# Weight blocks of three slots, with a new order of the head and of the whole list, in a hand-ordered 3x3 convolution with max pooling

## The chip, the cores and the metric

The kernel runs on one core of a Trainium2 chip. The metric is the device time of one execution in microseconds (us). Three runs of the kernel before took 105.31 to 105.68 us, with a median of 105.47.

## The reference

`x` is 16 x 64 x 64 x 64 (batch, input channels, rows, columns), `weight` is 128 x 64 x 3 x 3, both float32. The output is 16 x 128 x 32 x 32.

```python
x_pad = np.pad(x, ((0, 0), (0, 0), (1, 1), (1, 1)))
for b, co, ci, kh, kw:
    conv[b, co] += weight[co, ci, kh, kw] * x_pad[b, ci, kh:kh+h, kw:kw+w]
output[b, c, i, j] = np.max(conv[b, c, 2*i:2*i+2, 2*j:2*j+2])
```

## The kernel before

**Two ways to make a pair of rows.** The maximum of two neighbouring convolution rows is needed, and the kernel saves matmuls by working on sums and differences of input rows. The work is cut into 32 units: eight pairs of images (two images of 64 channels fill the 128 partitions), four quarters of the height each, eight output rows to a quarter. `SEQ` (line 37) makes 13 of them "K" units and 19 "W" units. A K unit reads bfloat16 rows (`kx`) and needs one row sum (`ks`). A W unit reads float32 rows (`wx`) and needs four row operations that cast as they add or subtract: `we`, `wz`, `wy`, `ws`.

**Products.** A product (line 214) is three matmuls, one for each kernel column, over eight rows of 64 columns, for one image of the pair. It reads 64 partitions (half of the array's rows) with a weight block `wt`, and the products of the two halves (h = 0 and 1) are issued in turn, so that they run side by side in the array. A K unit has the products PAa and PAb into one PSUM bank, PBa and PBb into another, and PR into the second; a W unit has P2 and P0 into one bank, and P3 and P1 into a second one. The names ending in x or a (PAx.0, P1a.18) are half-height parts of the first and the last product. There are eight PSUM banks (`acc`), handed out by number in the list: `PAa.1.0:7` takes bank 7 for unit 1, half 0.

**After the products.** For a K unit ScalarE copies the first bank out (EV), VectorE takes the row maximum with the second (MX), PR adds the common part, ScalarE copies the odd columns out (OD), and VectorE takes the column maximum with the even ones (CM) and stores. For a W unit ScalarE first writes the negated first bank into the second one (SE, line 295), before P0 adds to the first; then ev, mx, P1, od and cm follow in the same way. Row operations are KS (sum of `kx` rows), E or e (`we` on VectorE or on GpSimd), Z (`wz`), Y (`wy`), both on GpSimd, and S (`ws`, VectorE). GpSimd's row operations and some of its other work are held behind the last VectorE operation that reads SBUF alone (`on_gpsimd`, line 81).

**The weights.** `weight` lands as `wraw` (128 output channels on the partitions). From its three kernel rows g0, g1, g2 the head makes seven blocks in bfloat16 in `wq`: D2 = g2 - g1, D0 = g0 - g1, G0, G1, G2, and GM and GP, which are (g0 + g2 - g1) and (g0 + g2 + g1), halved later. TensorE transposes each (`turn`, line 160) into a PSUM bank, and `turn_out` (line 170) copies it to `wt` (on ScalarE line 176, on VectorE lines 178 and 180). A block has four slots of 64 columns, the first one zero, and is turned by four full transposes, each of two neighbouring slots, so that the lower 64 partitions of `wt` hold slot j - 1 and the upper 64 hold slot j; the matmul of half h for kernel column kw therefore reads slot kw - h (line 204).

**Loads.** SyncE's queue carries `wraw`, the first 17 rows of `x` for K unit 0 (`kfirst`, in two parts), the first rows of W unit 0 (`wx`, behind a warm-up matmul), then `ksecond`, the rows of K unit 1 (step KX2, held until D2 is done), further `wx` rows (LD.1 behind GM, LD.2 behind E.0, LD.3 behind E.1, and so on), and the stores. GpSimd's queue carries later K rows (steps L0 to L5, L0 behind KS.0). `kfirst` and `ksecond` are float32 and are cast into `kx`: XO1, XO and XE for the first, X1 (odd rows, needed by PAa.1) and X2 (needed by PBa.1) for the second.

**The order.** Nothing schedules at run time: `ORDER` (line 428) lists every step of all engines as one sequence, and each engine runs its own steps in that order, waiting where data or a bank is missing. `/V`, `/A` and `/P` name VectorE, ScalarE and GpSimd. Two products joined with + are issued matmul by matmul in turn; this text calls such a pair a step of TensorE. Eight warm-up matmuls of 512 columns (line 490) run before the first transpose.

Of the kernel before, what the change touches and what calls it, by code (L numbers as in the profile page):

```python
# [10 lines left out]
def kernel(  # L11
# [8 lines left out]
    nc = tc.nc  # L20
# [109 lines left out]
        nc.gpsimd.memset(t[:, 0, :], 0.0)  # L130
        nc.gpsimd.memset(t[:, H + 1, :], 0.0)

    D2, G0, D0, G2, GM, G1, GP = range(1, 29, 4)
    BLOCKS = {"D2": D2, "G0": G0, "D0": D0, "G2": G2, "GM": GM, "G1": G1, "GP": GP}
    wq = const.tile([CO, 29, CI], BF16)
    wt = const.tile([128, 28, CO], BF16)
    gsum = const.tile([CO, 3, CI], FP32)
    for s in range(0, 29, 4):
        nc.gpsimd.memset(wq[:, s, :], 0.0)
    wv = wraw.rearrange("a (c k) -> a k c", k=K * K)  # L140
    g0, g1, g2 = wv[:, 0:3, :], wv[:, 3:6, :], wv[:, 6:9, :]

# [11 lines left out]
    turned = {}  # L154


    def turned_rows(m):
        return acc.bitcast(BF16)[:, turned[m]]

    def turn(m, bank):  # L160
        t = turned[m] = take(bank)
        unset.add(t)
        for j in range(4):
            nc.tensor.transpose(  # L164
                turned_rows(m)[:, j, :],
                wq[:, BLOCKS[m] - 1 + j : BLOCKS[m] + 1 + j, :].rearrange("a b c -> a (b c)"),
                ident,
            )

    def turn_out(m, engine):  # L170
        free.add(turned[m])
        src = turned_rows(m)[:, 0:4, :]
        dst = wt[:, BLOCKS[m] - 1 : BLOCKS[m] + 3, :]
        half = m in ("GM", "GP")
        if engine is nc.scalar:
            nc.scalar.mul(dst, src, 0.5) if half else nc.scalar.copy(out=dst, in_=src)
        elif half:
            nc.vector.tensor_scalar_mul(out=dst, in0=src, scalar1=0.5)
        else:
            nc.vector.tensor_copy(out=dst, in_=src)  # L180
# [12 lines left out]
    def taps(dst, h, m0, rows, start=False, skip=None, part=(0, R)):  # L193
        lo = h * CI
        i0, i1 = max(part[0], int(skip == 0)), min(part[1], R - int(skip == R - 1))
        made = []
        for kw in (1, 0, 2):
# [3 lines left out]
            made.append(  # L201
                lambda kw=kw, o0=o0, o1=o1, c0=c0, c1=c1: nc.tensor.matmul(  # L202
                    dst[:, i0:i1, o0:o1],
                    wt[lo : lo + CI, m0 + kw - h, :],
                    rows(lo, i0, i1, c0, c1),
                    start=start and kw == 1,
                    stop=True,
# [211 lines left out]
    for name, f in ("ev", evac), ("mx", rowmax), ("od", odd), ("cm", colmax):  # L419
# [6 lines left out]


    ORDER = """
        D0/V g2 g1/P D2 g0 TD0:1 GS/V TD2:4 KX2 XO1/A TG1:0 VD2/V TG0:2 GP/V XO/A TG2:3 VG0/A
        PAx.0.0:6+PAx.0.1:7 GM/V PAa.0.0+PAa.0.1 VD0/A VG1/V LD.1 PAb.0.0+PAb.0.1 XE/V VG2/A TGM:2 KS.0  # L430
        TGP:4 E.0 VGM/A PBa.0.0:0+PBa.0.1:1 EV.0.0 Z.0 VGP/V LD.2 PBb.0.0+PBb.0.1 EV.0.1 P2.0.0:4+P2.0.1:3
        X1/A S.0 L0 PAa.1.0:7+PAa.1.1:2 SE.0.1:5 MX.0.0 Y.0 SE.0.0:6 PAb.1.0+P0.0.1 MX.0.1 X2/A
        P0.0.0+PAb.1.1 E.1 EV.1.0 PR.0.0+PR.0.1 ev.0.1 S.1 LD.3 EV.1.1 PBa.1.0:7+P3.0.1 KS.1 Z.1 OD.0.1
        P2.1.0:2+PBa.1.1:3 OD.0.0 CM.0.1 ev.0.0 mx.0.1 P3.0.0+PBb.1.1 SE.1.0:4 Y.1 PBb.1.0+P2.1.1:1 MX.1.1
        P0.1.0+P1.0.1 CM.0.0 e.2 MX.1.0 SE.1.1:0 P3.1.0+PR.1.1 LD.4 mx.0.0 ev.1.0 PR.1.0+P0.1.1 Y.2 LD.5
        OD.1.1 mx.1.0 od.0.1 P1.0.0+P3.1.1 OD.1.0 CM.1.1 ev.1.1 P1.1.0+P2.2.1:2 cm.0.1 Z.2 od.0.0 mx.1.1
        PAa.2.0:5+PAa.2.1:3 SE.2.1:1 CM.1.0 PAb.2.0+PAb.2.1 L1 od.1.0 cm.0.0 KS.3 PBa.2.0:7+PBa.2.1:6 EV.2.1
        E.3 LD.6 PBb.2.0+P0.2.1 EV.2.0 S.2 LD.7 P2.2.0:3+P1.1.1 KS.2 ev.2.1 Z.3 cm.1.0 PAa.3.0:5+PBb.2.1
        od.1.1 MX.2.0 SE.2.0:2 PAb.3.0+P3.2.1 cm.1.1 Y.3 MX.2.1 PR.2.0+P2.3.1:4 EV.3.0 mx.2.1
        P0.2.0+PAa.3.1:0 OD.2.0 S.3 P2.3.0:5+P1.2.1 ev.2.0 CM.2.0 e.4 P3.2.0+PAb.3.1 od.2.1 SE.3.1:3 cm.2.1  # L440
        PBa.3.0:7+PR.2.1 mx.2.0 SE.3.0:1 Z.4 PBb.3.0+P0.3.1 OD.2.1 P0.3.0+P3.3.1 CM.2.1 ev.3.1 MX.3.0 Y.4
        P1.2.0+PBa.3.1:6 ev.3.0 LD.8 mx.3.1 P2.4.0:4+PBb.3.1 EV.3.1 E.5 od.2.0 PR.3.0+P1.3.1 SE.4.0:5 KS.4
        cm.2.0 P3.3.0+PAa.5.1:0 Y.5 OD.3.0 MX.3.1 od.3.1 P0.4.0+PAb.5.1 mx.3.0 P3.4.0+PR.3.1 Z.5 cm.3.1
        ev.4.0 P1.3.0+P2.4.1:2 EV.5.1 mx.4.0 OD.3.1 PAa.4.0:3+PAa.4.1:4 L2 S.4 SE.4.1:0 PAb.4.0+PAb.4.1
        od.3.0 CM.3.0 Y.6 CM.3.1 P1.4.0+P0.4.1 EV.4.0 cm.3.0 P2.5.0:6+P3.4.1 LD.9 od.4.0 S.5 EV.4.1
        PBa.4.0:3+P2.5.1:7 cm.4.0 e.7 ev.4.1 PBb.4.0+PBa.4.1:1 mx.4.1 SE.5.0:2 PAa.5.0:4+PBb.4.1 SE.5.1:5
        KS.5 MX.4.0 PAb.5.0+P1.4.1 e.6 MX.4.1 P0.5.0+P0.5.1 EV.5.0 PR.4.0+P3.5.1 S.6 ev.5.1 Z.6
        P3.5.0+P2.6.1:4 ev.5.0 mx.5.1 od.4.1 PBa.5.0:7+PR.4.1 OD.4.0 mx.5.0 Y.7 PBb.5.0+P1.5.1 CM.4.0 OD.4.1
        CM.4.1 P1.5.0+PBa.5.1:6 od.5.1 MX.5.0 Z.8 SE.6.1:3 P2.6.0:1+PBb.5.1 cm.4.1 od.5.0 PR.5.0+P0.6.1
        cm.5.0 Z.7 MX.5.1 LD.10 SE.6.0:2 PAa.6.0:0+P3.6.1 cm.5.1 ev.6.1 PAb.6.0+PR.5.1 OD.5.0 e.8 mx.6.1  # L450
        P0.6.0+P2.7.1:4 OD.5.1 EV.6.0 CM.5.1 P3.6.0+PAa.6.1:5 CM.5.0 SE.7.1:0 PAa.7.0:6+PAb.6.1 KS.6 ev.6.0
        S.8 P2.7.0:7+P0.7.1 EV.6.1 S.7 PAb.7.0+P1.6.1 ev.7.1 mx.6.0 L3 PBa.6.0:1+P3.7.1 EV.7.0 Y.8
        P1.6.0+P2.8.1:5 od.6.1 mx.7.1 SE.7.0:4 PBb.6.0+PBa.6.1:6 cm.6.1 od.6.0 e.9 cm.6.0 SE.8.1:3
        P0.7.0+PBb.6.1 MX.6.0 P2.8.0:2+P1.7.1 ev.7.0 LD.11 Z.10 MX.6.1 PR.6.0+P0.8.1 LD.12 SE.8.0:7 LD.13
        P3.7.0+PR.6.1 od.7.1 S.9 ev.8.1 P0.8.0+P3.8.1 Z.9 cm.7.1 mx.7.0 P3.8.0+PAa.7.1:5 ev.8.0 mx.8.1
        P1.7.0+PAb.7.1 OD.6.1 Y.9 OD.6.0 mx.8.0 P2.9.0:0+P1.8.1 EV.7.1 CM.6.0 e.10 P1.8.0+P2.9.1:2 CM.6.1
        od.8.1 SE.9.0:5 cm.8.1 PAa.9.0:1+PBa.7.1:6 SE.9.1:3 S.10 P0.9.0+PBb.7.1 od.8.0 KS.7 od.7.0
        P3.9.0+P0.9.1 cm.8.0 ev.9.0 Y.10 MX.7.1 PAb.9.0+P3.9.1 ev.9.1 mx.9.0 PBa.7.0:7+P2.10.1:0 EV.9.0 Z.11
        mx.9.1 P2.10.0:2+PR.7.1 SE.10.1:1 cm.7.0 PBb.7.0+P1.9.1 E.11 OD.7.1 P1.9.0+P0.10.1 LD.14 CM.7.1
        od.9.1 Z.12 MX.7.0 LD.15 PAa.8.0:4+P3.10.1 od.9.0 cm.9.1 ev.10.1 PR.7.0+PAa.8.1:6 S.11 SE.10.0:3  # L460
        PAb.8.0+PAb.8.1 Y.11 mx.10.1 OD.7.0 P3.10.0+P2.11.1:0 CM.7.0 EV.8.1 cm.9.0 P0.10.0+P1.10.1 L4 KS.8
        SE.11.1:6 S.12 PBa.8.0:7+PBa.8.1:5 ev.10.0 LD.16 E.12 PBb.8.0+P0.11.1 EV.8.0 LD.17 mx.10.0 od.10.1
        Y.13 P2.11.0:2+PBb.8.1 ev.11.1 MX.8.0 P1.10.0+P3.11.1 SE.11.0:4 cm.10.1 Y.12 PR.8.0+PAa.9.1:0 MX.8.1
        od.10.0 P0.11.0+P2.12.1:1 mx.11.1 OD.8.0 Z.13 cm.10.0 P3.11.0+PR.8.1 ev.11.0 CM.8.0
        P2.12.0:3+P1.11.1 OD.8.1 mx.11.0 e.13 SE.12.1:2 PBa.9.0:7+PAb.9.1 CM.8.1 od.11.1 P1.11.0+P3.12.1
        cm.11.1 EV.9.1 KS.9 PBb.9.0+P0.12.1 SE.12.0:6 S.13 od.11.0 P2.13.0:0+PBa.9.1:5 E.14 ev.12.1
        P0.12.0+PBb.9.1 Y.14 cm.11.0 SE.13.0:1 mx.12.1 P3.12.0+P2.13.1:4 ev.12.0 MX.9.1 Z.14 P0.13.0+P1.12.1
        SE.13.1:3 MX.9.0 P3.13.0+PR.9.1 ev.13.0 mx.12.0 e.15 PR.9.0+P0.13.1 OD.9.1 mx.13.0 P1.12.0+P3.13.1
        CM.9.1 OD.9.0 Y.15 ev.13.1 CM.9.0 P1.13.0+P2.14.1:0 od.12.1 mx.13.1 od.12.0 PAa.11.0:4+P2.15.1:5
        od.13.0 Z.15 cm.12.0 SE.14.1:7 PAb.11.0+P1.13.1 cm.12.1 cm.13.0 PAa.10.0:6+P0.14.1 od.13.1 E.16  # L470
        SE.15.1:1 PAb.10.0+P3.14.1 S.15 ev.14.1 P2.14.0:2+P0.15.1 EV.11.0 cm.13.1 S.14 L5 P2.15.0:0+P3.15.1
        ev.15.1 LD.18 e.17 mx.14.1 PBa.10.0:4+PAa.11.1:3 EV.10.0 mx.15.1 SE.14.0:5 PBb.10.0+PAb.11.1
        SE.15.0:6 S.17 P0.14.0+P1.14.1 EV.11.1 KS.10 P0.15.0+P1.15.1 Z.17 MX.10.0 ev.14.0 P3.15.0+PAa.10.1:3
        od.15.1 ev.15.0 cm.15.1 P3.14.0+PAb.10.1 Y.16 od.14.1 mx.15.0 PR.10.0+PBa.10.1:2 EV.10.1 mx.14.0
        Y.17 P2.17.0:0+PBb.10.1 OD.10.0 cm.14.1 P1.15.0+P2.16.1:3 SE.17.0:1 MX.10.1 Z.16 P1.14.0+PAa.12.1:7
        CM.10.0 od.15.0 cm.15.0 P0.17.0+PR.10.1 od.14.0 SE.16.1:4 cm.14.0 P2.16.0:6+PAb.12.1 ev.17.0 S.18
        PBa.11.0:5+P0.16.1 OD.10.1 KS.11 EV.12.1 P3.17.0+P2.17.1:0 S.16 SE.16.0:7 PBb.11.0+P3.16.1 CM.10.1
        e.18 ev.16.1 mx.17.0 P0.16.0+PBa.11.1:2 SE.17.1:3 MX.11.0 P1.17.0+PBb.11.1 Y.18 ev.16.0
        PR.11.0+P0.17.1 MX.11.1 od.17.0 P2.18.0:6+P3.17.1 Z.18 cm.17.0 ev.17.1 mx.16.1 P3.16.0+PR.11.1
        SE.18.0:1 mx.17.1 PAa.12.0:0+P1.16.1 OD.11.0 OD.11.1 KS.12 P0.18.0+P1.17.1 CM.11.1 od.16.1 CM.11.0  # L480
        P3.18.0+P2.18.1:2 cm.16.1 od.17.1 mx.16.0 ev.18.0 PAb.12.0+PBa.12.1:5 SE.18.1:4 mx.18.0
        PBa.12.0:6+PBb.12.1 EV.12.0 cm.17.1 PBb.12.0+P0.18.1 MX.12.1 P1.16.0+P3.18.1 MX.12.0 ev.18.1
        P1a.18.0+PR.12.1 od.16.0 mx.18.1 oda.18.0 cm.16.0 OD.12.1 P1.18.0+P1a.18.1 cma.18.0 PR.12.0+P1.18.1
        CM.12.1 od.18.0 oda.18.1 cm.18.0 od.18.1 cma.18.1 OD.12.0 cm.18.1 CM.12.0
    """

    ones = nc.const_aps.tensor(1.0, [128, 512], BF16)
# [68 lines left out]
```

## Time and profile before

| what | us |
|---|---|
| median of three runs | 105.47 |
| the profiled execution | 105.41 |
| its span | 103.6 |
| TensorE busy | 97.4 of 103.6 |
| VectorE, ScalarE, GpSimd busy | 90.7, 82.0, 67.0 |
| first product (PAx) starts | 6.08 |
| `ksecond` lands | 9.78 |
| PAa.1 starts | 10.47 |
| last product of the unbroken stream ends its part of the chain | 97.52 |

The profile is one execution on the chip, taken by the hardware profiler; times are from the start of its span. The profiled execution took 1.8 us more than its span. PE is TensorE's matmuls, PEld its weight loads, DVE is VectorE, ACT ScalarE, POOL GpSimd and SP SyncE. A row names the line of the kernel, the operation, what it writes <- what it reads with the shapes, how many there are, and in brackets the idle time before it and what ended it. Matmuls are pipelined: a matmul's row is drawn with the time its results take to leave the array, so neighbouring rows overlap, and the distance between two starts is the time that one takes from the other.

### The profile page before, as it was taken

To read this page: it belongs to the slowest core of one execution; us is meant where nothing else is said; L and a number is where in the kernel's file an instruction comes from. 1 tells how busy PE (TensorE), PEld (TensorE's weight loads), DVE (VectorE), ACT (ScalarE), POOL (GpSimd) and SP (SyncE) were. 2 spreads that over 40 slices of the span, in tenths; PEclk is the share of its full clock that TensorE was granted. 3 is DMA by queue.
4 is the path that set the end of the run, shared out by engine and by line. 5 is a ranking of instruction groups with operands and counts; after the bars stand their busy time and mean duration, and the time that the engine had idled before them with its cause. 6 is when DMAs were issued, how large, how long until landed. Compare 5 with 4: busy or idle time off the path is not lost.

```text
span 103.6 us, 2525 instructions
## 1 busy us (share of the span) xinstructions
PE 97.4 (94%) x894; PEld 57.1 (55%) x894; DVE 90.7 (87%) x180; ACT 82.0 (79%) x179; POOL 67.0 (65%) x76
## 2 busy tenths in 40 slices
PE   7998999999999999999999999999999999999920
PEld 2273555555765555555555665655555655666500
DVE  1599979998899899897998999989999999899960
ACT  4478986887988967799879879789889988988530
POOL 7306679847958769968795765984992696770000
PEclk9999999999999999999999999999999999999999
DMA  2976898799998996799899789999948913502362
GB/s 58 348 290 232 213 169 295 227 290 206 368 346 297 160 234 256 229 241 143 194 276 355 280 218 340 168 246 274 366 159 171 272 67 113 191 0 101 108 214 89
DMA packets 12925, 22.81 MB, mean 220 GB/s; under 512 B 1008, under 2 KB 9200, under 8 KB 12912
## 3 DMA queue, kind: packets, MB, share of 16 engines
q1 hardware_dynamic: 11904, 19.63, 56.0%
q0 software_dynamic: 864, 2.88, 19.1%
q8 instruction: 7, 0.11, 0.5%
q10 hardware_dynamic: 144, 0.13, 0.4%
q14 instruction: 6, 0.05, 0.2%
HBM read 17.14 MB, written 8.39 MB: 246 GB/s over the span
## 4 chain that ended last, share of the span: by engine, by line
PE 84%; DMA 7%; DVE 2%; ACT 1%; issue 1%; DVEq 0%
PE acc L202 84%; DMA ksecond<-in_x_dram 5%; DMA wraw<-in_weight_dram 3%; ACT od L304 1%; DVE o L328 1%; DVE wq L395 1%; ACT kx L352 1%; DVE wq L360 0%; DVEq L551 0%
## 5 line engine op out<-in xcount | busy, mean ns | idle before, releaser
L202 PEld LDWEIGHTS <-wt 64*128 64x128 bf16 x858 | 54.4, 94 | 37.3 <-issue 1.3
L202 PE MATMUL acc<-kx,wt 64*128 64x504 bf16 (+5 forms) x318 | 57.5, 369 | 0.4 <-ACT kx L352 0.4
L299 DVE TENSOR_TENSOR acc<-acc,ev 128x512 f32<-128x512 f32 x64 | 42.4, 693 | 3.2 <-PE acc L202 2.2
L290 ACT COPY ev<-acc 128x512 f32<-128x512 f32 x64 | 36.6, 592 | 6.2 <-PE acc L202 5.5
L260 POOL TENSOR_TENSOR wz<-wx 128x512 bf16<-128x512 f32 x19 | 24.1, 1270 | 10.6 <-DVE ks L260 4.4
L202 PE MATMUL acc<-wy,wt 64*128 64x504 bf16 (+1 forms) x114 | 29.6, 377 | 0.0
L202 PE MATMUL acc<-wz,wt 64*128 64x504 bf16 (+1 forms) x114 | 29.2, 377 | 0.0
L202 PE MATMUL acc<-we,wt 64*128 64x504 bf16 (+1 forms) x114 | 29.1, 377 | 0.0
L260 POOL TENSOR_TENSOR wy<-wx 128x512 bf16<-128x512 f32 x19 | 24.1, 1270 | 7.8 <-PE acc L202 3.1
L202 PE MATMUL acc<-ws,wt 64*128 64x504 bf16 (+3 forms) x120 | 28.8, 366 | 0.1
L328 DVE TENSOR_TENSOR o<-acc,od 128x256 f32<-128x256 f32 (+1 forms) x66 | 25.6, 409 | 2.8 <-ACT od L304 2.2
L304 ACT COPY od<-acc 128x256 f32<-128x256 f32 (+1 forms) x66 | 23.3, 375 | 4.5 <-PE acc L202 2.9
L295 ACT ACTIVATE acc<-acc 128x512 f32<-128x512 f32 x38 | 22.0, 586 | 3.4 <-DVE o L328 1.9
L202 PE MATMUL acc<-ks,wt 64*128 64x504 bf16 (+1 forms) x78 | 19.8, 377 | 0.0
L260 POOL TENSOR_TENSOR we<-wx 128x512 bf16<-128x512 f32 x11 | 14.0, 1269 | 5.1 <-PE acc L202 3.4
L260 DVE TENSOR_TENSOR ws<-wx 128x512 bf16<-128x512 f32 x19 | 15.0, 792 | 0.0
L260 DVE TENSOR_TENSOR we<-wx 128x512 bf16<-128x512 f32 x8 | 6.1, 768 | 0.0
L260 DVE TENSOR_TENSOR ks<-kx 128x512 bf16<-128x512 bf16 x13 | 5.4, 419 | 0.1
L105 POOL DMA_DIRECT2D kx<-in_x_dram x6 | 3.5, 589 | 0.0
L490 PE MATMUL acc<-const-bfloat16-1.0 128*128 128x512 bf16 x6 | 2.7, 623 | 0.8 <-PEq L537 0.8
L360 DVE TENSOR_TENSOR wq<-wraw 128x192 bf16<-128x192 f32 x1 | 0.5, 500 | 2.6 <-DMA wraw<-in_weight_dram 2.6
L164 PEld LDWEIGHTS <-wq 128*128 128x128 bf16 x28 | 1.7, 102 | 1.7 <-issue 1.0
(28 smaller groups left out, 18.5 us busy)
## 6 DMA issues: line engine op xcount, KB each, us to landing
out_dram<-o SPq DMA_DIRECT2D x30, 256.0 KB, 4.5
wx<-in_x_dram SPq DMA_DIRECT2D x9, 512.0 KB, 6.6
wx<-in_x_dram SPq DMA_DIRECT2D x5, 480.0 KB, 6.4
wx<-in_x_dram SPq DMA_DIRECT2D x4, 544.0 KB, 6.3
kx<-in_x_dram POOLq DMA_DIRECT2D x3, 496.0 KB, 8.0
kx<-in_x_dram POOLq DMA_DIRECT2D x2, 528.0 KB, 8.9
wx<-in_x_dram SPq DMA_DIRECT2D x1, 576.0 KB, 10.1
ksecond<-in_x_dram SPq DMA_DIRECT2D x1, 512.0 KB, 4.7
```

Source lines behind the costliest of these rows:

```text
L105: return nc.gpsimd.dma_start(out=ktile(i)[:, lo:hi, :], in_=rows_of(p, lo, hi))
L164: nc.tensor.transpose(turned_rows(m)[:, j, :], wq[:, BLOCKS[m] - 1 + j : BLOCKS[m] + 1 + j, :].rearrange("a b c -> a (b c)"), ident,)
L202: lambda kw=kw, o0=o0, o1=o1, c0=c0, c1=c1: nc.tensor.matmul(dst[:, i0:i1, o0:o1], wt[lo : lo + CI, m0 + kw - h, :], rows(lo, i0, i1, c0, c1),
L260: return engine.tensor_tensor(out=r, in0=t[:, f + a : f + a + 2 * R - 1 : 2, :], in1=t[:, f + b : f + b + 2 * R - 1 : 2, :], op=op,)
L290: nc.scalar.copy(out=ev[g], in_=acc[:, ta[g]])
L295: nc.scalar.mul(acc[:, t], acc[:, ta["w", i, h]], -1.0)
L299: nc.vector.tensor_tensor(out=t, in0=t, in1=ev.pop(g), op=MAX)
L304: nc.scalar.copy(out=od[g][:, part], in_=acc[:, tb[g], part, 1::2])
L328: nc.vector.tensor_tensor(out=o[:, h, part], in0=acc[:, tb[g], part, 0::2], in1=od[g][:, part], op=MAX,)
L352: nc.scalar.copy(out=out, in_=in_)
L395: "D2", on_vector(nc.vector.tensor_sub(out=slots(D2), in0=g2, in1=g1))
L490: warm = nc.tensor.matmul(acc[:, n], src[:, 0:128], src, start=True, stop=True, skip_group_check=True)
```

## The change

The blocks of `wq` and `wt` have three slots instead of four, and no zero slot; the memsets of the zero slots on GpSimd are gone. Two full transposes write slots 0 and 1 of a turned block (lower half slot j, upper half slot j + 1). The third slot is made by two transposes of 64 columns: one puts slot 2 into the lower 64 partitions, the other puts slot 0 into the upper 64. A matmul of half 1 reads slot (kw - 1) mod 3. `turn_out` copies 384 columns instead of 512.

```diff
-    D2, G0, D0, G2, GM, G1, GP = range(1, 29, 4)
+    D2, G0, D0, G2, GM, G1, GP = range(0, 21, 3)
...
-    wq = const.tile([CO, 29, CI], BF16)
-    wt = const.tile([128, 28, CO], BF16)
+    wq = const.tile([CO, 21, CI], BF16)
+    wt = const.tile([128, 21, CO], BF16)
...
-    for s in range(0, 29, 4):
-        nc.gpsimd.memset(wq[:, s, :], 0.0)
...
-        for j in range(4):
+        rows, b = turned_rows(m), BLOCKS[m]
+        for j in 0, 1:
             nc.tensor.transpose(
-                turned_rows(m)[:, j, :],
-                wq[:, BLOCKS[m] - 1 + j : BLOCKS[m] + 1 + j, :].rearrange("a b c -> a (b c)"),
-                ident,
+                rows[:, j, :], wq[:, b + j : b + j + 2, :].rearrange("a b c -> a (b c)"), ident
             )
+        nc.tensor.transpose(rows[0:CI, 2, :], wq[:, b + 2, :], ident)
+        nc.tensor.transpose(rows[CI:, 2, :], wq[:, b, :], ident)
...
-        src = turned_rows(m)[:, 0:4, :]
-        dst = wt[:, BLOCKS[m] - 1 : BLOCKS[m] + 3, :]
+        src = turned_rows(m)[:, 0:3, :]
+        dst = wt[:, BLOCKS[m] : BLOCKS[m] + 3, :]
...
-                    wt[lo : lo + CI, m0 + kw - h, :],
+                    wt[lo : lo + CI, m0 + (kw - h) % 3, :],
```

The list `ORDER` is new throughout. Its head, before and after, up to the second step behind PAa.1:

```diff
-        D0/V g2 g1/P D2 g0 TD0:1 GS/V TD2:4 KX2 XO1/A TG1:0 VD2/V TG0:2 GP/V XO/A TG2:3 VG0/A
-        PAx.0.0:6+PAx.0.1:7 GM/V PAa.0.0+PAa.0.1 VD0/A VG1/V LD.1 PAb.0.0+PAb.0.1 XE/V VG2/A TGM:2 KS.0
-        TGP:4 E.0 VGM/A PBa.0.0:0+PBa.0.1:1 EV.0.0 Z.0 VGP/V LD.2 PBb.0.0+PBb.0.1 EV.0.1 P2.0.0:4+P2.0.1:3
-        X1/A S.0 L0 PAa.1.0:7+PAa.1.1:2 SE.0.1:5 MX.0.0 Y.0 SE.0.0:6 PAb.1.0+P0.0.1 MX.0.1 X2/A
+        g1/A D2 D0/V g0 KX2 TD2:2 TG1:0 XO1/V g2 VD2/V TG0:1 GS/V TG2:3 VG0/A XO/V PAx.0.0:6+PAx.0.1:7 GP/P
+        VG1/V XE/A TD0:2 PAa.0.0+PAa.0.1 VD0/A GM/V TGP:1 PAb.0.0+PAb.0.1 KS.0 LD.1 VGP/A E.0 TGM:0 VG2/A
+        PBa.0.0:4+PBa.0.1:2 Z.0 VGM/A LD.2 EV.0.1 PBb.0.0+PBb.0.1 EV.0.0 P2.0.0:1+P2.0.1:3 L0 X1/V MX.0.1
+        SE.0.0:5 PAa.1.0:6+PAa.1.1:0 Y.0 SE.0.1:7 MX.0.0 P0.0.0+PAb.1.1 X2/A S.0 PR.0.0+PR.0.1 EV.1.1 E.1
```

So g1 moves from GpSimd to ScalarE, GP from VectorE to GpSimd, XO1, XO and X1 from ScalarE to VectorE, XE from VectorE to ScalarE; D2 comes ahead of D0; TD0 moves behind PAx, and TGP and TGM stand between products of K unit 0, where before they stood together. In the rest of the list the same products, row operations and evacuations stand in another order and in other banks; of the 19 `we` row operations VectorE has nine (eight before) and GpSimd ten (eleven before). At the end ScalarE's queue issues two of the last stores and SyncE's the others; before it was one.

## The prediction

> **What bounds the kernel now.** I read the page first (busy shares, then the chain that ended last), then the whole chain in order of time, then the timeline of the first 11 us. The page:
>
> ```profile
> span 103.6 us, 2525 instructions
> PE 97.4 (94%) x894; PEld 57.1 (55%) x894; DVE 90.7 (87%) x180; ACT 82.0 (79%) x179; POOL 67.0 (65%) x76
> PE 84%; DMA 7%; DVE 2%; ACT 1%; issue 1%; DVEq 0%
> ```
>
> TensorE is the bound, and the chain in order of time (start, length, what) shows where it is not:
>
> ```profile
> 0.74 3.02 DMA wraw<-in_weight_dram
> ...
> 3.78 0.50 DVE wq L360
> 4.28 0.76 DVE wq L395
> ...
> 5.05 4.72 DMA ksecond<-in_x_dram
> ...
> 9.80 0.63 ACT kx L352
> ...
> 10.47 87.05 PE acc L202 x801
> ```
>
> From 10.47 us TensorE runs 87.05 us without a wait. The changed kernel puts the same matmuls into that stretch, so the result hangs on when it begins and on whether a wait opens in it. Ahead of it: the weights land at 3.76, VectorE makes D0 and only then D2, the load KX2 is held until D2 is done (5.05), lands at 9.78, ScalarE casts it (X1), and PAa.1 starts. TensorE's timeline of that stretch:
>
> ```profile
> 4.42 0.49 PE L164 MATMUL acc<-ident,wq 128*128 128x128 bf16 x4
> 5.08 1.07 PE L164 MATMUL acc<-ident,wq 128*128 128x128 bf16 x16 [0.17 <-DVE wq L395]
> 6.08 1.40 PE L202 MATMUL acc<-kx,wt 64*128 64x256 bf16 x18
> 7.42 0.62 PE L164 MATMUL acc<-ident,wq 128*128 128x128 bf16 x8
> 7.97 1.47 PE L202 MATMUL acc<-kx,wt 64*128 64x512 bf16 x12
> 9.28 0.81 PE L202 MATMUL acc<-we,wt 64*128 64x512 bf16 x6
> 10.47 0.39 PE L202 MATMUL acc<-kx,wt 64*128 64x512 bf16 x2 [0.38 <-ACT kx L352]
> ```
>
> Rows are drawn with their drain, so I read starts, not lengths. A transpose lasts 0.22, so the sixteen start from 5.08 to 5.93: 0.057 apart. The step from the last transpose (5.93) to the first product (6.08) is 0.15, and from 7.82 (the end of the eight less 0.22) to 7.97 again 0.15. Back again it is 7.13 (the last product of 0.19 pitch) to 7.42. So each change between the full array (128*128) and half-row tiles (64*128) costs 0.09 to 0.10 beyond the pitch. P2.0, begun at 9.28, could hand over at 9.93; PAa.1 starts at 10.47: 0.54 is lost to the landing.
>
> **The change, part by part.** Times continue the profiled execution (span 103.6, 105.41 in all; the runs' median is 105.47, 0.06 more).
>
> *D2 first, KX2 earlier.* The two weight differences on VectorE:
>
> ```profile
> 3.78 0.50 DVE L360 TENSOR_TENSOR wq<-wraw 128x192 bf16<-128x192 f32 x1 [2.65 <-DMA wraw<-in_weight_dram]
> 3.81 0.85 POOL L391 CAST wq<-wraw 128x192 bf16<-128x192 f32 x1 [1.29 <-DMA wraw<-in_weight_dram]
> 4.20 0.83 DVE L395 TENSOR_TENSOR wq<-wraw 128x192 bf16<-128x192 f32 x1
> ```
>
> D2 now comes first and is done at 4.28; KX2 goes out at 4.30, 0.75 earlier. It stands in SP's queue behind the same transfers, so I take its landing 0.75 earlier too, at 9.03; at worst it stays at 9.78, since data of the transfer ahead still lands at 7.32. The second difference took 0.83 while POOL cast g1, against 0.50 alone; g1 is now ScalarE's, so D0 ends near 4.70. X1 moves to VectorE: by the 576-element cast (0.48) some 0.43, at worst ScalarE's 0.61. It is done at 9.5 (worst 10.4). VectorE has nothing to do then but the row maxima of K unit 0.
>
> *Transposes.* Each of the seven weight blocks had four full transposes. It now has two full ones and two of 64 columns, one into each half of the partitions. Such a half is a tile of 128*64, a form that the trace doesn't hold. The nearest row is the change between 128*128 and 64*128, 0.15 from start to start, and the two halves of one form start 0.01 apart there (the paired products at 6.08). A block then costs 0.06 + 0.15 + 0.01 + 0.15 = 0.37 until the next form starts, against 0.23. The ends: no change of form at all, 0.19; nothing side by side, 0.41. I take 0.37.
>
> The Trainium skill, "TensorEngine Tiling (Array Packing)", Key Properties, says that a change of tiling mode, not of the tile alone, drains the TensorE. The 0.15 at 6.08 and 7.97 agrees for row tiles; no run here yet shows column tiles. It speaks against this edit: by it every block pays two drains.
>
> *TensorE up to PAa.1.* TD2 starts at 4.42 as TD0 did (the warm-up matmuls end there). The first block of before took 0.11 more than the pitch, 4.42 to 4.70 for three steps; kept: 0.48, to 4.90. TG1, TG0 and TG2 at 0.37: 5.27, 5.64, 6.01. Their casts on ScalarE (three at a pitch of 0.44 from 3.78, the last done at 5.18) are in time, and so is VD2 on VectorE: XO1 ends at 4.9, 384 columns instead of 512 take 0.32 of 0.42, done near 5.4. PAx starts at 6.01, against 6.08: the 0.66 saved by D2 first is spent on the form changes. From there come the products of before, 1.24 (6.08 to 7.32) and 1.96 (7.97 to 9.93), and between them TD0, TGP and TGM, each 0.10 in and 0.37 out: 1.41. Before had only eight transposes there, 0.65. PAa.1 is reached at 6.01 + 1.24 + 1.96 + 1.41 = 10.62, after X1 (9.5). The wait of 0.54 is gone, and TensorE's own work has taken its place, 0.15 later than before.
>
> *A new wait behind PAa.1.* In before the step after PAa.1 began with PAb.1.0. Now it begins with P0.0.0, which needs SE.0.0 on ScalarE, which needs the end of P2.0.0. P2.0 starts at 9.97; its last matmul starts 0.43 later and lasts 0.38: 10.78. SE at 0.58 (L295) and 0.05 to hand over: 11.43. TensorE could start at 11.27, so it waits 0.16, and all behind it. In before the second step started at 11.12. From there both run the same work: **+0.31**.
>
> *What stays covered.* Evacuations of 384 columns save ScalarE about 0.1 each (0.59 at 512, 0.40 at 256); VD0, VG2 and VGM end some 0.7 to 1.3 us before their products, so it counts nothing; without that cover each would cost its 0.5. GP on POOL starts at 5.75 (GS done) and takes between 0.48 (1.27 by size) and 0.85 (the cast): 6.6 at the latest, TGP is due at 7.2. GM may wait for POOL as D2 did, so LD.1 goes out near 6.9 against 6.80; E.1, its reader, ran at 11.72 after a landing of 11.64 and is due by 14.0 (P2.1, four steps of 0.65 behind 11.43). POOL's memsets of wq (0.76) lay in a wait for the weights: nothing. E0 no longer stands behind a late KS.0 and starts with its data at 7.35, so Z.0 and the POOL load L0 go out some 0.7 earlier, and LD.2 0.6.
>
> *The rest of the order.* VectorE gets nine of the 19 "we" rows instead of eight (0.77 each) and POOL ten instead of eleven (1.27). The densest stretch (54 to 76) has VectorE drawn busy 21.2 of 22, overlaps counted twice, and TensorE waited for it nowhere. The spacing of the list is alike: P2 to its P0 never under two steps behind unit 0, P3 to P1 never under two but at the end, PBb to PR never under two, in both. I count 0; at the ends -0 (no wait is there to take away) and +0.65, one step lost. In the tail the last stores change queues, with two on ScalarE's (0.37 an issue) instead of one; the last still follows the last column maximum: 0 to +0.1, taken as 0.
>
> Sum: 105.41 + 0.31 = 105.72, as a median some 0.06 more: **105.75**.
>
> **Rivals.**
> 1. *Half transposes cost no change of form* (faster). A block at 0.23 or less: TG2 then waits for its cast, 5.23, and PAx starts at 5.55; 1.24 + 1.96 + three blocks of 0.10 + 0.32 bring PAa.1 to 10.0. SE.0.0 still holds the second step, to 10.8, against 11.12: 105.1; with the halves side by side 104.95. It decides below about 0.04 a change. For it: the change has the same count of matmuls, and the landing no longer holds. Against it: every change of form in the trace cost 0.09.
> 2. *Weight loads of the halves aren't hidden* (slower). The load on wq lasts 102 ns, hidden under a pitch of 57. One uncovered per block adds 0.045 x 7 = 0.3: 106.1. It decides as soon as a block passes 0.41. For it: a load after a change of form (7.41) began only when the products had left. The Trainium skill, same page, Restrictions, says that column tiling disables Fast Weight Load; no run here shows it.
> 3. *One step is lost in the stream* (slower): a load or a seed is late somewhere in the new list, +0.65: 106.4. For it: many loads are issued at other places of the list, and the DMA engines are 0.9 busy from 10 to 76 us (the stretches' DMA share). Against it: the same spacing ran 87 us without a wait.
> 4. *The change does only half of it*: one form change per block is hidden, 105.4.
>
> **Chances.** Forecast 0.42 (its own range 105.55 to 105.95), rival 1 0.28, rival 2 0.12, rival 3 0.10, rival 4 0.08. 0.3% is 0.32 us, about what a measurement of this kernel can tell from no change. The forecast lies at that bound, so I halve it: slower 0.21 + 0.12 + 0.10 = 0.43; same 0.21 + 0.06 = 0.27; faster 0.28 + 0.02 = 0.30. The range takes in rivals 1, 2 and 4, and ends short of most of rival 3: 104.9 to 106.25.
>
> **What would show it.** Half transposes starting 0.15 after the full ones; PAx at 6.0 and not 5.55; PAa.1 released by nothing but TensorE's own queue near 10.6; the second step near 11.4, behind an ACT seed; ksecond landing near 9.0. I am wrong if the halves follow at 0.06, if ksecond lands after 10.1, or if the chain shows a wait after 12 us.

## The result and the profile after

The changed kernel took 106.74 us (median), the kernel before 105.76 in the runs beside it: a ratio of 1.0103 [1.0074, 1.0133]. It is slower by about 1.0 us, three times what was forecast, and outside the range. Executions more than 1.5% longer than the fastest of their kernel (two of the seven here, three of the six of e5 below) are counted in the medians and left out of the ratios. The profiled execution of the changed kernel took 106.74 as well, 1.33 more than that of before (105.41). The page after:

```profile
span 105.0 us, 2514 instructions
PE 99.0 (94%) x894; PEld 53.0 (50%) x894; DVE 91.4 (87%) x181; ACT 81.0 (77%) x179; POOL 65.0 (62%) x67
PE 85%; DVE 6%; POOL 2%; ACT 2%; issue 1%; DVEq 0%
```

The busy shares say nothing. The last line, the chain by engine, does: the landing (DMA, 7% before) is gone, and VectorE and GpSimd have 8% of it. The chain in order of time (start, length, what) says where:

```profile
8.90 2.70 PE acc L202 x24
...
11.62 5.41 PE acc L202 x48
...
20.40 0.82 DVE ws L260
21.22 0.34 DVE ks L260
21.56 0.60 DVE we L260
...
22.42 0.42 DVE o L328
...
22.88 4.74 PE acc L202 x42
...
28.90 1.27 POOL wy L260
30.17 1.24 POOL wz L260
...
31.45 67.11 PE acc L202 x618
```

Before, TensorE had one piece of 87.05 us from 10.47. Now the stream is broken twice behind the head: at 22.88 and at 31.45 it starts again, released by VectorE and by GpSimd. The chain's long way back over other engines is not lost time; from the starts of TensorE's own matmuls, each of the two waits is 0.23. A third, 0.08, is at 93.39. The steps that wait are PAa.3.0+PBa.2.1, for the bank that cm.1.0 frees on VectorE, P0.4.0+PR.3.1, for Z.4 on GpSimd, and PAa.12.0+P1.16.1. (The list of waits shows none of them: a matmul's row is drawn with its drain, longer than such a wait.)

TensorE's timeline of the head, with a block of transposes and the first products behind it:

```profile
5.31 0.29 PE L164 MATMUL acc<-ident,wq 128*128 128x128 bf16 x2
5.53 0.24 PE L167 MATMUL acc<-ident,wq 128*64 128x128 bf16 x1
5.53 0.24 PE L168 MATMUL acc<-ident,wq 128*64 128x128 bf16 x1
5.71 0.28 PE L164 MATMUL acc<-ident,wq 128*128 128x128 bf16 x2
...
6.10 0.50 PE L202 MATMUL acc<-kx,wt 64*128 64x256 bf16 x6
...
10.79 0.81 PE L202 MATMUL acc<-kx,wt 64*128 64x512 bf16 x6
11.62 0.39 PE L202 MATMUL acc<-wz,wt 64*128 64x512 bf16 x1
```

A block now lasts from 5.31 to 5.71, 0.40: the second full transpose starts at 5.38, the halves 0.15 later and together, the next block 0.18 later. PAx starts at 6.10, PAa.1 at 10.79 with nothing but TensorE ahead of it, the second step at 11.62, 0.19 later than TensorE alone would allow.

The lag of the changed kernel against before, step by step: +0.32 at PAa.1, +0.51 at the second step (11.62 against 11.11), +0.75 behind 22.88, +0.97 behind 31.45, +1.04 at the last matmul, and +1.33 at the end of the span (104.96 against 103.63). So the terms are 0.51 in the head, 0.53 in the stream (its three waits) and 0.29 in the tail.

The tail, on ScalarE's timeline, before and after:

```profile
98.76 0.98 ACT L304 COPY od<-acc 128x128 f32<-128x128 f32 x4 [0.64 <-DVE o L328]
```

```profile
98.58 0.58 ACT L304 COPY od<-acc 128x128 f32<-128x128 f32 x2 [0.17 <-PE acc L202]
100.08 0.43 ACT L304 COPY od<-acc 128x128 f32<-128x128 f32 x2 [0.92 <-PE acc L202]
100.70 0.54 ACT L304 COPY od<-acc 128x128 f32<-128x128 f32 x2 [0.19 <-DVE o L328]
```

Before, four copies run as one row that begins under the last matmuls. After, oda.18.1 waits for the last matmul until 100.08, with od.18.0 behind it on the same queue, whose data were ready; the last two copies then wait for VectorE as well. From the end of the last matmul to the issue of the last store it is 1.36 before (98.99 to 100.35) and 1.70 after (100.03 to 101.73); to the end of the span 4.64 and 4.93, so that 0.29 of the 0.34 is left there.

### The profile page after: what moved, and what is told of

Same layout as the page of the kernel before. It is cut to its first block, busy times and chain, and to the rows that moved or that the text cites. A ratio compares the mean times of both kernels' runs of the same rounds, so it can differ in the third digit from the quotient of the medians.

```text
span 105.0 us, 2514 instructions
## 1 busy us (share of the span) xinstructions
PE 99.0 (94%) x894; PEld 53.0 (50%) x894; DVE 91.4 (87%) x181; ACT 81.0 (77%) x179; POOL 65.0 (62%) x67
## 4 chain that ended last, share of the span: by engine, by line
PE 85%; DVE 6%; POOL 2%; ACT 2%; issue 1%; DVEq 0%
PE acc L202 79%; PE acc L490 3%; DVE o L328 3%; PE acc L164 2%; DVE ws L260 1%; ACT od L304 1%; PE acc L167 1%; POOL wy L260 1%; POOL wz L260 1%; ACT ev L290 1%; DVE we L260 1%; DVE acc L299 0%; DVE ks L260 0%; DVEq L299 0%; PE acc L168 0%
## 5 line engine op out<-in xcount | busy, mean ns | idle before, releaser
L202 PEld LDWEIGHTS <-wt 64*128 64x128 bf16 x858 | 50.2, 94 | 41.5 <-issue 1.3
L202 PE MATMUL acc<-kx,wt 64*128 64x504 bf16 (+5 forms) x318 | 54.1, 369 | 0.1
L290 ACT COPY ev<-acc 128x512 f32<-128x512 f32 x64 | 37.1, 593 | 7.5 <-PE acc L202 7.1
L202 PE MATMUL acc<-wy,wt 64*128 64x504 bf16 (+1 forms) x114 | 28.4, 377 | 0.0
L202 PE MATMUL acc<-we,wt 64*128 64x504 bf16 (+1 forms) x114 | 27.2, 377 | 0.0
L202 PE MATMUL acc<-ks,wt 64*128 64x504 bf16 (+1 forms) x78 | 18.1, 377 | 0.0
L260 POOL TENSOR_TENSOR we<-wx 128x512 bf16<-128x512 f32 x10 | 12.7, 1273 | 3.2 <-DVE ks L260 1.4
L260 DVE TENSOR_TENSOR ws<-wx 128x512 bf16<-128x512 f32 x19 | 13.9, 741 | 0.0
L260 DVE TENSOR_TENSOR ks<-kx 128x512 bf16<-128x512 bf16 x13 | 6.0, 466 | 0.1
L368 POOL TENSOR_TENSOR wq<-gsum,wraw 128x192 bf16<-128x192 f32 x1 | 0.7, 687 | 3.9 <-DVE gsum L364 3.9
```

The costliest lines, as they stand in the source:

```text
L202: lambda kw=kw, o0=o0, o1=o1, c0=c0, c1=c1: nc.tensor.matmul(dst[:, i0:i1, o0:o1], wt[lo : lo + CI, m0 + (kw - h) % 3, :], rows(lo, i0, i1 ...
L260: return engine.tensor_tensor(out=r, in0=t[:, f + a : f + a + 2 * R - 1 : 2, :], in1=t[:, f + b : f + b + 2 * R - 1 : 2, :], op=op,)
L290: nc.scalar.copy(out=ev[g], in_=acc[:, ta[g]])
L368: inst = engine.tensor_tensor(out=slots(m), in0=gsum, in1=g1, op=op)
```

## The experiments

**Theory:** three causes that add up: the halves' form changes in the head (about 0.4), the tail's order (0.3), and two waits that the new list opens in the stream (0.45). **Rivals:** (A) the waits are only a late head's consequence and go with it; (B) the halves are free and the whole loss is the list's. The experiments below separate the terms. Ratios of e1 to e12 are against the kernel before on the same chip (medians 105.34 to 105.36).

**e1: the blocks alone.** The list of before, blocks as in the change.

```diff
-        for j in range(4):
+        for j in 0, 1:
...
+        nc.tensor.transpose(rows[0:CI, 2, :], wq[:, b + 2, :], ident)
+        nc.tensor.transpose(rows[CI:, 2, :], wq[:, b, :], ident)
```

> The kernel before with the three-slot blocks alone, its list unchanged. Theory (a change of form costs 0.09 to 0.10, so a block takes 0.40 instead of 0.23): four blocks from 5.08 put PAx near 6.7 (6.08 before), two more blocks and the same products put PAa.1 near 10.8 (10.47), and the seed behind P2.0 holds the next step a little: +0.3 to +0.5 us against the kernel before. Rival (the half transposes cost nothing, the new list costs it all): PAx at 6.1, within 0.05 us of the kernel before.

Measured 105.78, 1.0039 [1.0019, 1.0058], so +0.41. Its chain has TensorE unbroken over the whole stream (until 97.89):

```profile
8.79 89.10 PE acc L202 x819
```

PAx starts at 6.60 and PAa.1 at 10.68. The blocks, placed as before placed them, cost 0.4 and open no long wait (the longest is 0.08). Rival B falls.

**e2: the list alone.** The new list with four-slot blocks (four full transposes).

```diff
-    D2, G0, D0, G2, GM, G1, GP = range(0, 21, 3)
+    D2, G0, D0, G2, GM, G1, GP = range(1, 29, 4)
...
-        for j in 0, 1:
+        for j in range(4):
```

> The new list with the four-slot blocks of the kernel before. Theory (form changes cost the head 0.7, and the new list itself holds two waits near 22.9 and 31.4 us, 0.45 together, and a tail 0.3 longer): PAx near 5.6, PAa.1 near 10.0, second step near 10.8, waits and tail as in the changed kernel: about +0.4 us against the kernel before, 0.7 faster than the change. Rival A (the waits in the stream come of the late head): they are gone, about 0.0. Rival B (half transposes cost nothing): as slow as the change, +1.1.

Measured 106.39, 1.0100 [1.0062, 1.0137]: about 1.05, where 0.4 was expected, a miss; it is the time that rival B forecast here, and only e1 speaks against that rival. In its profiled execution (105.88, the fastest of the six) the head is early, PAa.1 at 9.93 and the second step at 10.76, yet the waits of 0.23 stand at 22.03 and 30.60, at the same steps. They belong to the list and not to the late head: rival A falls. The early head of that one execution is not typical, as the repeat shows.

**e12: the same again.**

> The kernel of e2 again: its profiled execution was half a microsecond faster than the median of its runs. Theory (X1 on VectorE is lengthened in the executions in which Z.0 overlaps it): a profile near the median shows X1 near 1.0 us, PAa.1 0.2 to 0.4 late, and VectorE's waits after it; near 105.9 it shows X1 at 0.43 again. Rival (the spread is the clock's or the loads'): X1 is 0.43 in a slow profile too.

Measured 106.40, 1.0089 [1.0060, 1.0117]. The profiled execution (106.48) has the same waits (0.23, 0.22, 0.08) and the same tail; the 0.60 between the two profiles lies in the head. PAx starts at 6.06 instead of 5.45 and the second step at 11.38 instead of 10.76. The trace records TensorE's clock at full from 5.97 us here, from 3.87 in e2. VectorE's cast X1 isn't the cause: 0.53 here, 0.43 there. So the list, taken alone, gains nothing in its head on the average, and loses its waits and its tail. The waits and the tail make about 0.8 of its 0.94 to 1.05.

**e3: the changed kernel with the tail of before.**

```diff
-        P1a.18.0+PR.12.1 mx.18.1 od.16.0 oda.18.0 cm.16.0 OD.12.1 P1.18.0+P1a.18.1 CM.12.1 PR.12.0+P1.18.1
-        oda.18.1 cma.18.0 od.18.0 cma.18.1 od.18.1 cm.18.0 OD.12.0 cm.18.1 CM.12.0
+        P1a.18.0+PR.12.1 mx.18.1 od.16.0 oda.18.0 cm.16.0 OD.12.1 P1.18.0+P1a.18.1 cma.18.0
+        PR.12.0+P1.18.1 CM.12.1 od.18.0 oda.18.1 cm.18.0 od.18.1 cma.18.1 OD.12.0 cm.18.1 CM.12.0
```

> The changed kernel with the last nine evacuations in the order of the kernel before (od.18.0 ahead of oda.18.1, cma.18.0 ahead of CM.12.1). Theory (oda.18.1 waits for the last matmul and od.18.0 stands behind it): from the last matmul's end to the last store's issue 1.35 us instead of 1.67, 0.3 us faster than the change, +0.8 against the kernel before. Rival (the tail's length is the stores' and not this order's): no difference to the change.

Measured 106.62, 1.0121 [1.0086, 1.0157]; against the change run again (e6, 1.0134) the times can't tell 0.3. The profiles can: 106.44 against 106.74, with PAa.1 at 10.77 and 10.79 and the last matmul starting at 99.63 and 99.66.

**e8: the kernel before with the tail of after,** the same edit the other way round, where nothing else moves.

> The kernel before with the last evacuations in the order of the changed kernel. Theory (od.18.0 stands behind oda.18.1, which waits for the last matmul): 1.67 us from the last matmul's end to the last store's issue instead of 1.36, +0.3 us against the kernel before. Rival: no difference.

Measured 105.56, 1.0026 [1.0013, 1.0039], so +0.27, where the traces of before and after differ by 0.34 at the last store's issue and by 0.29 at the end of the span. The tail's term is shown.

**e4: the changed kernel without halves.** The third slot is filled by two more full transposes, so it holds wrong weights; the work of the other engines stays.

```diff
-        for j in 0, 1:
+        for j, slot in (0, 0), (1, 1), (2, 1), (2, 1):
...
-        nc.tensor.transpose(rows[0:CI, 2, :], wq[:, b + 2, :], ident)
-        nc.tensor.transpose(rows[CI:, 2, :], wq[:, b, :], ident)
```

> The changed kernel with two full transposes (slots 1 and 2 again) in place of the two half ones, so that the third slot of wt holds wrong weights: the count of transposes, the copies of 384 columns and the list stay, and no change of form is left inside a block. Theory: a block takes 0.23 to its successor and 0.32 to a product, PAx near 5.6, second step near 10.8: 0.7 us faster than the change, +0.4 against the kernel before. Rival (the form is free and the separate places of TD0, TGP and TGM cost the head): no difference to the change.

Measured 106.26, 1.0090 [1.0062, 1.0117]. PAx starts at 5.43, 0.67 earlier than in the change; not all of that need be the forms', since TensorE's clock was full from 4.75 us here and from 5.28 there. Then PAa.1 waits 0.31 for X1, and the stream loses 0.30 at 17.71 to 18.31 and 0.28 and 0.23 at 22.47 and 31.05. The last matmul starts at 99.25, against 99.66: 0.41 of the 0.67 is left, and the rest goes where the earlier head runs into the work of VectorE and GpSimd.

**e5: the two waits mended,** by their place in the queue: cm.1.0 ahead of E.3 and KS.3, CM.1.1 ahead of KS.3, Z.4 ahead of Y.5.

```diff
-  KS.2 EV.2.0 E.3 PBb.2.0+P0.2.1 OD.1.1 EV.2.1 KS.3 P2.2.0:4+P3.2.1 Y.3 cm.1.0 od.1.1 CM.1.1 ev.2.1
+  KS.2 EV.2.0 cm.1.0 E.3 PBb.2.0+P0.2.1 OD.1.1 EV.2.1 P2.2.0:4+P3.2.1 CM.1.1 KS.3 Y.3 od.1.1 ev.2.1
...
-  LD.7 mx.3.1 Y.5 P0.3.0+PBa.3.1:0 od.2.0 EV.3.1 cm.2.0 P2.4.0:7+PBb.3.1 MX.3.0 Z.4
+  LD.7 mx.3.1 Z.4 P0.3.0+PBa.3.1:0 od.2.0 EV.3.1 cm.2.0 P2.4.0:7+PBb.3.1 MX.3.0 Y.5
```

> The changed kernel with two places of its list mended: cm.1.0 and CM.1.1 ahead of E.3 and KS.3 on VectorE, Z.4 ahead of Y.5 on POOL. Theory (the two waits of 0.23 at 22.9 and 31.4 us are made by the list itself): both gone and nothing in their place, 0.45 us faster than the change. Rival (VectorE is behind in this stretch whatever the order, its sums slowed by POOL): the waits turn up a few steps later, no gain.

Measured 107.58, 1.0121 [1.0098, 1.0143]; no gain. Its profiled execution had TensorE at full clock only from 9.78 us. On TensorE's timeline the same two transposes take 0.39 before that instant and 0.28 after it:

```profile
8.54 0.39 PE L164 MATMUL acc<-ident,wq 128*128 128x128 bf16 x2
...
10.10 0.28 PE L164 MATMUL acc<-ident,wq 128*128 128x128 bf16 x2
```

PAa.1 came at 12.44. Such an execution says nothing of the two waits, so it was repeated.

**e6: the change again,** the same kernel, beside e5.

> The changed kernel once more, beside the others on the same chip: both theories expect +1.0 to +1.2 us against the kernel before, the waits at 22.9 and 31.4 again if the list makes them, at other places if landings do.

Measured 106.96, 1.0134 [1.0108, 1.0161]. Waits at the same three steps (23.05, 31.62, 93.56: 0.22, 0.23, 0.08), PAa.1 at 10.96. The places are the list's, not one execution's.

**e11: e5 again.**

> The kernel of e5 again, whose profiled execution had its head stretched to PAa.1 at 12.4 us. Theory (list's order): with the head as in the change, no waits at 22.9 and 31.4, the last matmul 0.45 earlier. Rival (VectorE is behind whatever the order): waits of 0.2 to 0.5 at other places between 22 and 33 us.

Measured 106.84, 1.0133 [1.0091, 1.0174]. Both waits are gone, and one of 0.48 stands between them (0.45 before the mending). The chain:

```profile
27.16 1.65 DVE ws L260
28.80 0.61 DVE acc L299
...
29.65 0.70 DVE acc L299
...
30.39 67.75 PE acc L202 x624
```

VectorE's row operation ws takes 1.72 (1.65 of it in the chain) instead of 0.69, and the row maxima that PR.3.0 needs stand behind it. The rival of e5 and e11, that the wait only moves, holds: with either order something in that stretch is late. So the list's 0.46 there is read from the traces, and no run has won it back.

**e10: the list with all four named places mended** (four-slot blocks, X1 back on ScalarE, the two waits as in e5, the tail of before).

```diff
-  P2.0.0:1+P2.0.1:3 L0 X1/V MX.0.1
+  P2.0.0:1+P2.0.1:3 L0 X1/A MX.0.1
```

> The new list with four-slot blocks, X1 back on ScalarE, the two places of e5 and the tail of the kernel before. Theory (what the new list costs is X1 lengthened by Z.0 on GpSimd, VectorE's order near 22 us, GpSimd's near 31 us, and the tail): PAa.1 near 10.0, second step near 10.8, no wait after it but the one of every list near the end: -0.3 us against the kernel before. Rival (the list costs by its spacing everywhere): waits at other places, +0.3 or more.

Measured 106.53, 1.0100 [1.0067, 1.0133]. In the profile (105.96) the waits are 0.28 for X1 behind ScalarE's evacuations, 0.49 at 30.22, 0.09 at 91.52 and 0.08 at 92.89. The theory that four named places hold the list's loss falls; mended there, it loses elsewhere.

**e7: before with D2 first,** KX2 right behind it, TG2 ahead of TG1, and TD0 as the last of the five blocks ahead of PAx.

```diff
-  D0/V g2 g1/P D2 g0 TD0:1 GS/V TD2:4 KX2 XO1/A TG1:0
+  D2 KX2 g2 g1/P D0/V g0 TD2:4 TG2:3 GS/V XO1/A TG1:0
...
-  VD2/V TG0:2 GP/V XO/A TG2:3 VG0/A PAx.0.0:6+PAx.0.1:7
+  VD2/V TG0:2 GP/V XO/A TD0:1 VG0/A PAx.0.0:6+PAx.0.1:7
```

> The kernel before (four slots, its list) with D2 ahead of D0, KX2 right behind it and TD0 the last of the five blocks. Theory (0.54 of the head was the landing of ksecond): it lands some 0.45 earlier, PAx near 5.8, PAa.1 near 10.0 behind X1, nothing else moves: -0.4 us against the kernel before. Rival (the transfer ends when the DMA engines let it, whenever it is issued; or another wait takes its place): within 0.1.

Measured 105.14, 0.9986 [0.9968, 1.0003]. In the profiled execution (104.96, among the fastest of the twelve) ksecond lands at 8.98, 0.80 earlier, and PAa.1 starts at 9.75, 0.72 earlier, with 0.06 of a wait for X1. The last matmul is 0.53 earlier (98.09): 0.18 went back at 15.78, at P3.1.0+PR.1.1. P3.1.0 reads `wy`, which GpSimd had just made (Y.1, done at 15.73):

```profile
14.46 1.27 POOL L260 TENSOR_TENSOR wy<-wx 128x512 bf16<-128x512 f32 x1
...
15.78 0.37 PE L202 MATMUL acc<-wy,wt 64*128 64x512 bf16 x1
```

Ahead of Y.1 stands Z.1, held until VectorE's KS.1 is done, and VectorE was late there, its S.0 having taken 1.71 beside GpSimd's Z.0. The direction of the landing's part of the change is right in the profile; in the times it isn't clearly told from no change.

The landing's size isn't 0.80. In the six profiles with D0 first (the four of before, e1, e8) ksecond is issued at 4.85 to 5.05 and lands at 9.26 to 9.78; in the eleven with D2 first it is issued at 4.00 to 4.23 and lands at 8.98 to 9.59. The issue is some 0.8 earlier, the landing by its mean 0.25 (9.23 against 9.48). The profile from which the prediction took its 9.78 has the latest landing of all.

**e9: e7 with S.0 behind MX.0.0,** to take that wait away.

```diff
-  P2.0.0:4+P2.0.1:3 X1/A S.0 L0 PAa.1.0:7+PAa.1.1:2 SE.0.1:5 MX.0.0 Y.0
+  P2.0.0:4+P2.0.1:3 X1/A L0 PAa.1.0:7+PAa.1.1:2 SE.0.1:5 MX.0.0 S.0 Y.0
```

> The kernel before with D2 first as in e7, and S.0 placed behind MX.0.0. Theory (S.0 took 1.71 us on VectorE because GpSimd's Z.0 ran at the same time, and this backlog gave 0.18 of the gain back at P3.1.0+PR.1.1): S.0 near 0.7 us, no wait near 15.8, 0.2 faster than e7, -0.4 against the kernel before. Rival (the wait is ScalarE's or a landing's): the wait stays, -0.2 as e7.

Measured 105.42, 1.0004 [0.9984, 1.0025], a miss. S.0 took 0.68, as expected, but the wait is at the same step, P3.1.0+PR.1.1, and has grown: 0.48 at 16.82, again behind Y.1 (done at 16.76). Y.0, held behind S.0, now ran beside E.1, which took 1.39 on VectorE, and KS.1, Z.1 and Y.1 came later. The profiled execution was the slowest of the twelve (105.95), with full clock only from 6.66 us and PAa.1 at 10.49, so the size of this wait may not be typical.

**e13, e14, e15: the kernel before, profiled three times more,** to see what a late clock does to its head. Each is one execution.

> The kernel before once more, for its profile alone. Theory: its head ends with the landing of ksecond, so PAa.1 stays near 10.47 us (between 10.3 and 10.7) whenever TensorE's clock is raised up to about 5.5 us, and PAx moves with the clock (6.08 at a raise of 4.69). Rival: PAa.1 moves with PAx one for one, as it does in the kernels whose head is TensorE's own work (PAx 5.45 and PAa.1 9.93 at a raise of 3.87, 6.06 and 10.55 at 5.97).

> The kernel before a second time, for another instant of the clock's raise. Theory: PAa.1 near 10.47 us while its wait for the landing (0.38 and 0.54 with the handover) shrinks by as much as PAx is late. Rival: PAa.1 one for one with PAx.

> The kernel before a third time. Theory and rival as in the two looks ahead: PAa.1 near 10.47 us, or one for one with PAx.

| kernel before | full clock from | PAx | ksecond lands | wait ahead of PAa.1 | PAa.1 | second step |
|---|---|---|---|---|---|---|
| e15 | 3.41 | 5.88 | 9.54 | 0.51 | 10.23 | 10.87 |
| first profile | 4.69 | 6.08 | 9.78 | 0.54 | 10.47 | 11.11 |
| e14 | 5.70 | 6.29 | 9.61 | 0.17 | 10.30 | 10.94 |
| e13 | 6.43 | 6.61 | 9.32 | 0.05 | 10.50 | 11.14 |

PAx moves by 0.73 with the clock, PAa.1 by 0.27 and not in the same order; 10.23 is a little below the 10.3 expected, since ksecond landed at 9.54 there. The wait for the landing takes up the clock's lateness. In e12 against e2 (2.10 us between the two clocks) the second step moved by 0.62, as much as PAx. So the theory holds as far as these profiles go, in which the landing moves too: a head that is TensorE's own work hands a late clock on. The chain of e13 shows one thing more:

```profile
8.56 56.35 PE acc L202 x519
...
65.05 0.69 DVE acc L299
...
65.78 32.26 PE acc L202 x293
```

A wait of 0.40 for a row maximum stands at 65.78, in the kernel before, which in its other profiles shows 0.03 or nothing there. This execution took 105.94, the other two 105.35. The step that waits in e7 and e9, P3.1.0+PR.1.1, also waits in e15 (0.13), e14 (0.07) and e8 (0.25), each time behind Y.1: in the kernel before, too, an early head gives some of its lead back there.

## Why the prediction was wrong, step by step

- **D2 first, KX2 earlier:** right in direction, wrong in size. KX2 went out at 4.08, 0.97 earlier, and landed at 9.34, 0.44 earlier (9.03 forecast); over all profiles it is 0.25 (e7). It was no longer on the path. X1 ended at 10.46, not 9.5, beyond the worst case of 10.4, still 0.33 ahead of PAa.1.
- **Transposes, 0.37 a block:** right; 0.39 to 0.40 measured at full clock, in the order of its parts. The skill's rule (the Trainium skill, "TensorEngine Tiling (Array Packing)", Key Properties), that a change of mode drains the array, agrees for column tiles too, in that each change costs time: 0.15 in, 0.18 out, against a pitch of 0.057. Whether the array is empty at a change the rows can't show, since the ends of matmuls are modelled. Rivals 1 and 4 fall with it (e1), and rival 2 by its own mark, since a block stays under 0.41; why the way out is 0.18 and not 0.15 isn't shown. (The load at 7.41, named for rival 2, began 0.07 before the products' rows end, not behind them.)
- **TensorE up to PAa.1, 10.62:** 10.79. Of the 0.17, 0.09 were there at PAx, and that it is so little is luck: the weights had landed 0.23 earlier, so that TD2 began at 4.14 and not 4.42, and the four blocks took 1.96 and not 1.59, the first two 0.60 and 0.57 until the clock was full at 5.28 (4.69 in the profile of before). The rest is 0.02 a block.
- **A new wait behind PAa.1, 0.16:** 0.19, behind ScalarE's seed as forecast. (Its terms, 10.78 + 0.58 + 0.05, make 11.41 and not 11.43, and the second step of before began at 11.11, so the sum as written is +0.30.) The term **+0.31** of the head came out as +0.51 in that execution, and as +0.69 in that of e6, with full clock from 5.84.
- **"The rest of the order. I count 0":** this step failed. The stream lost 0.53: 0.23 in each of two places and 0.08 in a third. Even spacing of the products was taken to mean that no wait opens. The spacing of TensorE's steps is one condition; the other is what stands ahead of the freeing step in VectorE's and GpSimd's own queues. cm.1.0, which frees bank 3, stood behind S.2, KS.2, E.3 and KS.3; Z.4 stood behind Y.5, 1.27 us. Rival 3 named a lost step and put 0.65 on it with a chance of 0.10; its kind was right, its odds were not.
- **"What stays covered":** the evacuations and GP were covered as forecast. E0 did not start some 0.7 earlier: its rows landed at 8.06 (7.32 before), it began at 8.08 (7.95 before), and Z.0, behind it, lay under X1 (8.91 to 10.18). X1's price had been taken from a cast without such a neighbour, 0.43 to 0.48.
- **"In the tail ... 0 to +0.1, taken as 0":** failed, 0.29 in the profile and 0.27 by e8. It counted the queue that issues the stores and not the copies ahead of them: a copy that waits for the last matmul was put in front of one that could run.

So the sum 0.31 should have been 0.51 + 0.53 + 0.29 = 1.33, the difference of the two profiles. Two causes are shown by a run of their own, e1's 0.41 [0.20, 0.61] and e8's 0.27 [0.14, 0.41]; the third, 0.52 to 0.54 of waits, is read at the same three steps in the profiles of the change, e2, e3, e6 and e12. Together they make 1.20 to 1.22; the change measured 1.0103 and, again, 1.0134 [1.0108, 1.0161], that is 1.1 and 1.4. The single terms needn't add up exactly: in e4 0.26 of the 0.67 won in the head went back in the stream.

What stays open: which order, if any, keeps the earlier landing without a wait later. e7 has the best median, yet no version was clearly faster than before. What decides when ksecond lands, if its issue moves the landing so little, wasn't tested. How often a wait like that of 65.78 falls into the kernel before isn't known from four profiles.

## What to carry to other kernels

When a hand-ordered list is changed, go through each engine's own queue, not only the bound one's: for every step that frees a bank or makes an operand, sum what now stands ahead of it there. Part of an earlier start at the head may be given back at the next queue that is behind: 0.26 of 0.67 in e4, 0.19 of 0.72 in e7. Don't take one profile's landing for the rule: the 0.54 of wait that the change was to remove was the longest of four profiles. In the tail, no copy that must wait for the last matmul belongs ahead of one that needn't.

## What the runs showed of the hardware

**VectorE beside GpSimd.** In these traces a VectorE operation that reads SBUF alone was stretched by a GpSimd row operation under way when it started. VectorE's timeline after, X1 and S.2:

```profile
9.37 1.09 DVE L354 CAST kx<-ksecond 128x512 bf16<-128x512 f32 x1 [0.59 <-DMA ksecond<-in_x_dram]
...
20.32 0.91 DVE L260 TENSOR_TENSOR ws<-wx 128x512 bf16<-128x512 f32 x1
```

GpSimd's at the same time, Z.0 and Z.2:

```profile
8.91 1.27 POOL L260 TENSOR_TENSOR wz<-wx 128x512 bf16<-128x512 f32 x1 [2.52 <-DVE we L260]
...
19.39 1.29 POOL L260 TENSOR_TENSOR wz<-wx 128x512 bf16<-128x512 f32 x1
```

X1 took 1.09 and ended 0.28 behind Z.0; in e2, where Z.0 was over when it began, 0.43. It ended 0.28 to 0.29 behind Z.0 in the six other profiles in which the two overlap, whether it took 0.53 (e12) or 1.13 (e5). S.2 ended 0.55 behind Z.2; in e11 ws (27.08 to 28.80) ended 0.55 behind a wy of 26.99 to 28.25. It goes the other way too: in e11 GpSimd's `we` of 25.31, begun while a ws of VectorE ran (25.09 to 25.89), took 1.72 and not 1.27. The row maxima, which read PSUM, kept their mean of 693 ns. The Trainium skill, "SBUF — State Buffer", Who interferes with whom, has the two engines share a port pair as an exclusive lock; these rows agree in that VectorE does most of its work, 0.28 of X1's 0.43 and 0.55 of S.2's 0.69, once GpSimd is done.

**The clock's instant.** With the same kernel and program TensorE's clock was full from instants between 3.41 and 6.43 us in the four profiles of before, and from 9.78 in e5. The page's clock row shows 9 throughout; these are the instants at which the trace's own record of the clock begins, and at them the pitch of the full transposes falls from 0.107 to 0.056. The Trainium skill, "TensorE: Matmul & The Clock Gate", What's actually happening, says that the window is free-running and the change varies by 500 ns either way; these profiles differ from that, with 3.0 us between the earliest and the latest of one kernel.
